# Attention stage of a decoder trunk: block splits on VectorE, state-space parameters on GpSimd, q and k norms folded into later scales, head products by weight block

## The chip, the core and the metric

The kernel runs on one core of a Trainium2 chip. A core has five engines with an instruction queue each: TensorE (PE; its weight loads are listed apart as PEld), VectorE (DVE), ScalarE (ACT), GpSimd (POOL) and SyncE (SP), which here issues most of the loads. The engines run side by side and meet only at semaphores; on one engine the instructions run in the order in which the program has them. The metric is device time in microseconds (us), the median of several runs; lower is better.

## The reference

Two layers of a decoder trunk on 256 tokens of width 1024, in float32. The first layer is RMSNorm, one input projection, two groups of eight attention heads, an output projection and a residual, then a dense SwiGLU (width 3584). The second is a state-space layer (complex diagonal, 32 groups of 64 states), then a top-2-of-8 expert SwiGLU. The change touches the first layer's attention and the small tables of the state-space layer. The attention, cut down:

```python
h = _rms_norm(x, norm_g) @ w_in                    # columns: q, k, v of the stick-breaking heads | c_q 256 | c_kv 128 | k_rope 32
o_sb = stick_breaking(q, k, v)                     # 8 heads of 64, causal, scale 1/8
c_q, c_kv = _rms_norm(..., q_lat_g), _rms_norm(..., kv_lat_g)
q = (c_q @ w_q_up)                                 # 8 heads of 64 + 32 (rotary)
kv = (c_kv @ w_kv_up)                              # 8 heads of 64 (k) + 64 (v)
k = concat([kv[..., :64], k_rope shared by all heads])
q, k = _rms_norm(q, q_g), _rms_norm(k, k_g)        # over 96, per head, each with a gain of 96
q, k = _rope_tail(q, cos, sin), _rope_tail(k, cos, sin)   # last 32 of 96
o_mla = softmax(q k^T * 96 ** -0.5, causal) @ v
x + concat(o_sb, o_mla) @ w_out
```

The state-space layer needs, of 2048 pairs of numbers a, dt, the values exp(a dt) with cosine and sine and a quotient; they depend on weights alone.

## The kernel before

**Products by three.** A float32 operand is held as a high and a low part. `mm3` (L247 to L249) forms a product from three: high by high, high by low, low by high. A weight block (1 MB, 128 x 2048) is loaded into one of five raw buffers; `split` (L226 on) makes its two parts in two halves of 1024 columns: ScalarE casts the high part `wh` (L218), and the engine given as `sub` subtracts for the low part `wl` (L219, `wl = raw - wh`). The pairs stand in a ring of six, so a half's buffers are reused three blocks later, when TensorE has read them; a raw buffer is free, and the next load in SyncE's order may start, once both halves are split.

**The stage in order.** (1) x is transposed and split into `xh`, `xl`; the latent columns (c_q, c_kv, k_rope) are computed from four narrow blocks `wc` of 416 columns, into PSUM tiles `pav`. (2) `r0` is the reciprocal root of each token's mean square; `dg` (L380, GpSimd) is a diagonal of it, which a product with ones (L416) turns into the row `rb`. `setup_late` loads the tables `cat` (masks, cosines, sines, gains) and `spar` (parameters of the state-space layer). (3) The latents `csb` are normed (L386 to L397). `s5_first` computes the first tables of the state-space layer in a scratch tile `kp`; it contains two exponentials by polynomial (`exp_exact`, L899). (4) `heads_T` (L408) forms the stick-breaking q, transposed, in PSUM, four products of 128 rows in two calls; L418 scales it into `qT`. Between the calls the latents are transposed into `cT`. (5) For each half b of the tokens, L468 and L472 form q, k and v of the latent heads, ScalarE copies them into `qk` and `vkv`, squares are summed (L479, L480), `norm(b)` computes the reciprocal root (L256 to L273) and multiplies `qk` by it (L448) and by the gains (L450), and `rope(b)` rotates the last 32 columns (L459 to L462). (6) `heads_T` forms k into `kT`, around `norm(1)`; `qk_T(b)` (L490) transposes `qk` into `qkT`. (7) The values of the stick-breaking heads (L627) are formed in two halves of the weights, with the scores of the first two heads (L518, L519, L512) between.

(8) The loop of L635 runs the sixteen heads as a pipeline written by hand: in each turn it issues steps of several heads, with the lags of the table `LAG`. A latent head: scores and mask (L545, L546, L512), maximum (L549, L550) and its negative scaled (L551), exponential with row sums (L554, L555), division (L560 to L562), transposition (L567, L571) and product with v (L580). A stick-breaking head: L523 to L526, a sum (L530), products with a triangle (L534, L535), exponential (L539), L580. Pairs are merged into `mh`, `ml` (L586, L587). (9) `out(n, half)` multiplies by the output weights; then follow the residual and the dense layer.

**What sets the order.** There is no planner: each engine runs its instructions in the order of the code, and the scheduling is by hand. The PSUM tiles named `pw` share four buffers, `ptr` and `pav` two each; a product into a fifth `pw` waits until the first has been read. SyncE issues the weight loads in a fixed order, each when its buffer is free.

**Who splits.** Of the four `wc` blocks VectorE splits one and GpSimd three. Of the eight wide blocks up to the second output block VectorE splits the first two (q) and GpSimd the other six (two k, two v, two output): `split(g)` at L398, L432, L496, L499, L502 and L630. VectorE splits all later ones. `s5_first` runs on VectorE, `s5_second` on GpSimd behind the loop of step (8).

Of the kernel before, what the change touches and what calls it, by code (L numbers as in the profile page):

```python
# [8 lines left out]
F32 = mybir.dt.float32  # L9
# [40 lines left out]
C_W = C_QG + 192  # L50
# [44 lines left out]
def lay_out(i):  # L95
# [17 lines left out]
    par[:, C_QG:] = np.concatenate([i["att_q_norm"][0], i["att_k_norm"][0]])  # L113
# [24 lines left out]
class Net:  # L138
# [211 lines left out]
    def attention(self, kp):  # L350
# [4 lines left out]
        with ExitStack() as st:  # L355
# [26 lines left out]
            self.split(v)  # L382
# [15 lines left out]
            self.split(g)  # L398
# [3 lines left out]
            self.s5_first(kp)  # L402
# [4 lines left out]

            def heads_T(W, dst, sc, m2):  # L408
                pq = bank([P, 2, SEQ])
                for mi in range(2):  # L410
                    for k in range(KD):
                        wh, wl = W[k]
                        s = slice((2 * m2 + mi) * P, (2 * m2 + mi + 1) * P)
                        self.mm3(pq[:, mi], wh[:, s], wl[:, s], xh[:, k], xl[:, k], k == 0, k == KD - 1)
                if dst is qT and m2 == 0:
                    mm(pr, self.ones, dg, start=True, stop=True)  # L416
                    act.copy(rb, pr)
                v.scalar_tensor_tensor(out=dst[:, 2 * m2:2 * m2 + 2], in0=pq, scalar=sc,  # L418
                                       in1=rb.unsqueeze(1).to_broadcast([P, 2, SEQ]), op0=ALU.mult, op1=ALU.mult)
# [11 lines left out]
            heads_T(W, qT, 0.125, 1)  # L431
            self.split(g)  # L432
# [6 lines left out]
            qg = self.cat[:, C_QG - C_A:C_QG - C_A + 192].rearrange("p (a c) -> p a c", a=2)  # L439
# [4 lines left out]

            def norm(b):
                qk = qks[b]
                r = self.rsqrt(ssq[b], 16, 1.0 / 96, sm=a2)
                v.tensor_tensor(out=qk, in0=qk, in1=r.unsqueeze(2).to_broadcast([P, 16, 96]), op=ALU.mult)  # L448
                for n in range(2):
# [1328 lines left out]
```

## Time and profile before

| | us |
|---|---|
| median of 3 runs | 1320.66 (1320.35 to 1320.78) |
| profiled execution, its own time | 1320.32 |
| span in the trace | 1318.2 |
| PE / PEld busy | 1269.5 / 920.8 |
| DVE / ACT / POOL busy | 842.5 / 632.9 / 219.4 |

The rest of an execution, 2.1 us, lies around the span. In a row of the timeline stand the start, the time in us, the engine, the line and operation, out<-in with the partitions and elements, the count of merged instructions, and in brackets the idle time of the engine before it with what ended it. Consecutive PE rows overlap, since products are pipelined: the distance from start to start is the rate. A row of the windows has the stretch, its length with PE busy, then PEld, DVE, ACT and POOL busy with their counts, the granted clock of TensorE as a share of full speed, the share of DMA and GB/s. A row of the waits has who waited for whom, the total, the times and the longest.

### The profile page before, as it was taken

The numbers are of one execution on the slowest core, as the hardware profiler recorded it, in microseconds if no ns is written. First come the engines' busy times: TensorE is split into PE (matmuls) and PEld (weight loads), VectorE is DVE, ScalarE is ACT, GpSimd is POOL, SyncE is SP. The second block draws the span as 40 slices with busy tenths as digits, with TensorE's granted clock in tenths as the row PEclk, the third lists the DMA queues.
The fourth block names the chain that finished last, engine by engine and source line by source line (L and its number), as shares of the span: only waits on it lengthen the run. The fifth ranks groups of instructions, "written<-read, shape, count | busy, mean of one in ns | idle before, by whom it ended". The sixth has DMA issues, their size and how long they took to land.

```text
span 1318.2 us, 18472 instructions
## 1 busy us (share of the span) xinstructions
PE 1269.5 (96%) x6862; PEld 920.8 (70%) x6862; DVE 842.5 (64%) x1108; ACT 632.9 (48%) x825; POOL 219.4 (17%) x257
## 2 busy tenths in 40 slices
PE   7789999999998889999999999999999999999997
PEld 7566999999987778884357885346887436788433
DVE  6876886856788589981158984128987106898211
ACT  6345544444452457771047773026876105777100
POOL 4454598001724600000000000000000000000000
PEclk9889999999999989999999999999999999999999
DMA  8330654545553759999999999999999999999996
GB/s 303 133 123 17 227 220 161 189 168 187 192 191 134 268 195 372 375 343 384 416 418 418 417 419 416 417 418 418 418 417 419 418 418 417 418 418 418 416 419 246
DMA packets 66369, 421.22 MB, mean 320 GB/s; under 512 B 7504, under 2 KB 8784, under 8 KB 21472
## 3 DMA queue, kind: packets, MB, share of 16 engines
q1 hardware_dynamic: 65088, 418.15, 79.9%
q10 hardware_dynamic: 1008, 1.27, 0.3%
q8 instruction: 56, 0.92, 0.3%
q0 software_dynamic: 176, 0.56, 0.1%
q14 instruction: 41, 0.34, 0.1%
HBM read 418.89 MB, written 1.05 MB: 319 GB/s over the span
## 4 chain that ended last, share of the span: by engine, by line


## 5 line engine op out<-in xcount | busy, mean ns | idle before, releaser
L219 DVE TENSOR_TENSOR wl<-raw,wh 128x1024 fp32r<-128x1024 f32 (+1 forms) x427 | 516.2, 1245 | 100.2 <-ACT wh L218 85.8
L218 ACT CAST wh<-raw 128x1024 fp32r<-128x1024 f32 (+1 forms) x456 | 467.2, 1046 | 180.9 <-PE dn L249 63.0
L693 PE MATMUL pgu<-raw,we 128*64 128x512 f32 x896 | 203.6, 596 | 0.0
L247 PE MATMUL pgu<-wh,wy 128*128 128x512 f32 x448 | 178.2, 398 | 0.0
L248 PE MATMUL pgu<-wl,wy 128*128 128x512 f32 x448 | 174.6, 390 | 1.0 <-DVE wl L219 1.0
L249 PE MATMUL pgu<-wh,wy 128*128 128x512 f32 x448 | 174.8, 390 | 0.0
L693 PEld LDWEIGHTS pgu<-raw,we 128*64 128x64 f32 x896 | 61.0, 137 | 115.5 <-issue 113.8
L247 PE MATMUL pgu<-dxh,wh 128*128 128x256 f32 x448 | 127.2, 284 | 0.0
L249 PE MATMUL pgu<-dxh,wl 128*128 128x256 f32 x448 | 126.8, 283 | 0.0
L248 PE MATMUL pgu<-dxl,wh 128*128 128x256 f32 x448 | 126.7, 283 | 0.0
L247 PE MATMUL dn<-wh,gh 128*128 128x512 f32 x280 | 109.8, 392 | 0.0
L249 PE MATMUL dn<-wh,gl 128*128 128x512 f32 x280 | 109.1, 390 | 0.0
L248 PE MATMUL dn<-wl,gh 128*128 128x512 f32 x280 | 109.0, 389 | 0.0
L727 PE MATMUL dn<-raw,gh 128*64 128x512 f32 x448 | 101.9, 593 | 0.5 <-ACT gh L713 0.5
L247 PEld LDWEIGHTS pgu<-wh,wy 128*128 128x128 f32 x448 | 84.1, 188 | 23.8 <-issue 4.7
L249 PEld LDWEIGHTS pgu<-wh,wy 128*128 128x128 f32 x448 | 84.1, 188 | 18.1
L248 PEld LDWEIGHTS pgu<-wl,wy 128*128 128x128 f32 x448 | 84.2, 188 | 17.9 <-DVE wl L219 1.4
L704 DVE TENSOR_TENSOR sg<-pgu,sg 64x512 f32<-64x512 f32 x28 | 19.4, 693 | 110.9 <-ACT sg L703 110.9
L713 ACT COPY gh<-pgt 128x256 f32<-128x256 f32 x28 | 10.4, 372 | 163.4 <-PE pgt L711 163.4
L247 PEld LDWEIGHTS pgu<-dxh,wh 128*128 128x128 f32 x448 | 85.9, 192 | 0.5 <-issue 0.2
L248 PEld LDWEIGHTS pgu<-dxl,wh 128*128 128x128 f32 x448 | 86.0, 192 | 0.3
L249 PEld LDWEIGHTS pgu<-dxh,wl 128*128 128x128 f32 x448 | 85.9, 192 | 0.0
(414 smaller groups left out, 1666.0 us busy)
## 6 DMA issues: line engine op xcount, KB each, us to landing
raw<-in_wm_dram SPq DMA_DIRECT2D x292, 1024.0 KB, 15.0
raw<-in_wm_dram SPq DMA_DIRECT2D x88, 512.0 KB, 15.0
raw<-in_wd_dram SPq DMA_DIRECT2D x42, 1024.0 KB, 4.9
raw<-in_wqkv_dram SPq DMA_DIRECT2D x6, 1024.0 KB, 5.9
raw<-in_wo_dram SPq DMA_DIRECT2D x4, 1024.0 KB, 4.9
raw<-in_wglu_dram SPq DMA_DIRECT2D x4, 1024.0 KB, 4.9
raw<-in_ws_dram SPq DMA_DIRECT2D x2, 1024.0 KB, 4.6
raw<-in_wc_dram SPq DMA_DIRECT2D x4, 416.0 KB, 6.7
```

The source lines that it names most:

```text
L218: self.nc.scalar.copy(wh, w)
L219: (sub or self.sub).tensor_tensor(out=wl, in0=w, in1=wh.bitcast(F32), op=ALU.subtract)
L247: mm(out, sh, mh, start=start, stop=False)
L248: mm(out, sh, ml, start=False, stop=False)
L249: mm(out, sl, mh, start=False, stop=stop)
L693: nc.tensor.matmul(pg[64 * j:64 * j + 64], x(k), W[j][0][k % 4], start=(k == 0), stop=(k == KD - 1))
L704: v.tensor_tensor(out=sg[:64], in0=pg[64:], in1=sg[:64], op=ALU.mult)
L713: nc.scalar.copy(g, pt)
L727: nc.tensor.matmul(job["acc"][64 * n:64 * n + 64], gts[0][:, k], W[n][0][k], start=(f == 0 and k == 0), stop=(f == NF - 1 and k == 3))
```

## The change

1. Every split of the stage is VectorE's. The split of the second q block stands ahead of `r0`'s chain instead of behind it, that of the first value block ahead of `rope(0)`, and that of the second output block moves from between the value halves to turn 16 of the loop.
2. `s5_first` runs on GpSimd, without its reciprocal. Operations that multiply and add two tiles in one instruction are written as two there. `s5_second` is called after `norm(1)` instead of behind the loop; the reciprocal is its first step, on VectorE.
3. `heads_T` goes through the weights once: each of its eight row blocks serves all four head products in turn, in two PSUM tiles open together. The latents' transposes come after row blocks 7 and 8 of q, the product for `rb` after the fifth.
4. `norm(b)` multiplies only the k half by its reciprocal root. The q half's goes, with 96 ** -0.5, into the scale of the exponential (L554, L555) and into the maximum (two instructions for L551's one). The gains of the first 64 columns become the scale of ScalarE's copy in `qk_T`; those of the last 32 are multiplied into the cosine and sine tables once, by six small products on GpSimd in `setup_late`. `rope(b)` takes q and k apart: seven instructions for four.

The order of instructions in three places. First VectorE, from the polynomial to the first sums of squares; before (`kp` is the scratch tile of the state-space tables, `pw` the q heads' PSUM tile):

```order
L911 TENSOR_SCALAR kp<-kp 128x16
L913 SCALAR_TENSOR_TENSOR kp<-kp 128x16 x6
L914 TENSOR_SCALAR kp<-kp 128x16
L915 TENSOR_SCALAR kp<-kp 128x16
L916 TENSOR_TENSOR kp<-kp 128x16
L418 SCALAR_TENSOR_TENSOR qT<-pw,rb 128x512 x2
L475 COPY qk<-csb 128x8x32
```

and with the change, from the latents' scales on:

```order
L408 TENSOR_SCALAR csb<-csb,rr 128x128
L222 TENSOR_TENSOR wl<-raw,wh 128x1024 x2
L432 SCALAR_TENSOR_TENSOR qT<-pw,rb 128x512 x2
L222 TENSOR_TENSOR wl<-raw,wh 128x1024 x2
L499 COPY qk<-csb 128x8x32
```

The tables have gone from ahead of the q evacuation, and a k block's split stands on either side of it.

Second GpSimd, after the masks' casts; before, twelve halves of weight blocks and then `s5_second`:

```order
L310 CAST mib<-cat 128x128
L219 TENSOR_TENSOR wl<-raw,wh 128x1024 x12
L962 TENSOR_SCALAR kp<-kp 128x16
L963 TENSOR_SCALAR kp<-kp 128x16
L966 COPY kp<-kp 128x16
```

and with the change:

```order
L313 CAST mib<-cat 128x128
L320 TENSOR_TENSOR gc<-cat 128x64
L320 TENSOR_TENSOR gs<-cat 128x2x16 x2
L320 TENSOR_TENSOR gc<-cat 128x64
L320 TENSOR_TENSOR gs<-cat 128x2x16 x2
L929 TENSOR_SCALAR kp<-kp 128x16
L930 TENSOR_SCALAR kp<-kp 128x16
```

The splits have left this queue; the tables with gains and `s5_first` (L929 on, 50 instructions) stand in their place, with `s5_second` directly behind.

Third VectorE at the end of the loop; before:

```order
L560 RECIPROCAL rs<-rs 128x2
L561 TENSOR_SCALAR p<-p,rs 128x128
L562 TENSOR_SCALAR p<-p,rs 128x256
L571 COPY pT<-ptr 128x384
L587 TENSOR_TENSOR ml<-pav,mh 128x256
```

and with the change:

```order
L584 RECIPROCAL rs<-rs 128x2
L585 TENSOR_SCALAR p<-p,rs 128x128
L586 TENSOR_SCALAR p<-p,rs 128x256
L222 TENSOR_TENSOR wl<-raw,wh 128x1024 x2
L595 COPY pT<-ptr 128x384
L611 TENSOR_TENSOR ml<-pav,mh 128x256
```

The second output block's split has come between the last division and the last copies.

The diff, without context lines (the host part, which appends two columns of gains to the table `par`, left out):

```diff
--- before
+++ after
...
@@ -311,0 +315,8 @@
+        self.gc, self.gs = (pool.tile([P, 2, 2, 32], F32, name=nm) for nm in ("gc", "gs"))
+        qg = self.cat[:, C_QG - C_A:C_QG - C_A + 192].rearrange("p (a c) -> p a c", a=2)
+        for b in range(2):
+            for o, c, d, w, s_ in ((self.gc, C_COS, 0, 32, 64), (self.gs, C_SIN, 0, 16, 80), (self.gs, C_SIN, 16, 16, 64)):
+                c += 32 * b + d - C_A
+                nc.gpsimd.tensor_tensor(out=o[:, b, :, d:d + w], in0=self.cat[:, c:c + w].unsqueeze(1).to_broadcast([P, 2, w]),
+                                        in1=qg[:, :, s_:s_ + w], op=ALU.mult)
@@ -369 +380 @@
-                self.split(v if i == 0 else g)
+                self.split(v)
@@ -374,0 +386 @@
+            self.split(v)
@@ -383 +394,0 @@
-            self.split(v)
@@ -398 +409,2 @@
-            self.split(g)
+            self.s5_first(kp)
+            self.split(v)
@@ -402 +413,0 @@
-            self.s5_first(kp)
@@ -408,12 +419,15 @@
-            def heads_T(W, dst, sc, m2):
-                pq = bank([P, 2, SEQ])
-                for mi in range(2):
-                    for k in range(KD):
-                        wh, wl = W[k]
-                        s = slice((2 * m2 + mi) * P, (2 * m2 + mi + 1) * P)
-                        self.mm3(pq[:, mi], wh[:, s], wl[:, s], xh[:, k], xl[:, k], k == 0, k == KD - 1)
-                if dst is qT and m2 == 0:
-                    mm(pr, self.ones, dg, start=True, stop=True)
-                    act.copy(rb, pr)
-                v.scalar_tensor_tensor(out=dst[:, 2 * m2:2 * m2 + 2], in0=pq, scalar=sc,
-                                       in1=rb.unsqueeze(1).to_broadcast([P, 2, SEQ]), op0=ALU.mult, op1=ALU.mult)
+            def heads_T(dst, sc, between=None):
+                pq = [bank([P, 2, SEQ]) for _ in range(2)]
+                for k in range(KD):
+                    if k % 4 == 0:
+                        W = self.takek(4, 0)
+                    wh, wl = W[k % 4]
+                    for m in range(4):
+                        s = slice(m * P, (m + 1) * P)
+                        self.mm3(pq[m // 2][:, m % 2], wh[:, s], wl[:, s], xh[:, k], xl[:, k], k == 0 and m % 2 == 0, k == KD - 1 and m % 2 == 1)
+                    if between:
+                        between(k)
+                for m2 in range(2):
+                    v.scalar_tensor_tensor(out=dst[:, 2 * m2:2 * m2 + 2], in0=pq[m2], scalar=sc,
+                                           in1=rb.unsqueeze(1).to_broadcast([P, 2, SEQ]), op0=ALU.mult, op1=ALU.mult)
@@ -421,2 +434,0 @@
-            W = self.takek(4, 0) + self.takek(4, 0)
-            heads_T(W, qT, 0.125, 0)
@@ -424 +436,8 @@
-            for b in range(2):
+            def latents_T(k):
+                if k == 4:
+                    mm(pr, self.ones, dg, start=True, stop=True)
+                    act.copy(rb, pr)
+                if k < 6:
+                    return
+                b = k - 6
@@ -431,2 +450,3 @@
-            heads_T(W, qT, 0.125, 1)
-            self.split(g)
+            heads_T(qT, 0.125, latents_T)
+            self.split(v)
@@ -439 +458,0 @@
-            qg = self.cat[:, C_QG - C_A:C_QG - C_A + 192].rearrange("p (a c) -> p a c", a=2)
@@ -444,0 +464,3 @@
+            rq = [ap.tile([P, 16], F32, name=f"rq{b}") for b in range(2)]
+            SC = 96 ** -0.5
@@ -446,6 +468,6 @@
-                qk = qks[b]
-                r = self.rsqrt(ssq[b], 16, 1.0 / 96, sm=a2)
-                v.tensor_tensor(out=qk, in0=qk, in1=r.unsqueeze(2).to_broadcast([P, 16, 96]), op=ALU.mult)
-                for n in range(2):
-                    v.tensor_tensor(out=qk[:, 8 * n:8 * n + 8], in0=qk[:, 8 * n:8 * n + 8],
-                                    in1=qg[:, n].unsqueeze(1).to_broadcast([P, 8, 96]), op=ALU.mult)
+                self.rsqrt(ssq[b], 16, 1.0 / 96, rq[b], sm=a2)
+                k = qks[b][:, 8:]
+                v.tensor_tensor(out=k, in0=k, in1=rq[b][:, 8:].unsqueeze(2).to_broadcast([P, 8, 96]), op=ALU.mult)
+                v.tensor_scalar(out=rq[b][:, :8], in0=rq[b][:, :8], scalar1=SC, scalar2=None, op0=ALU.mult)
@@ -453,0 +476,9 @@
+                qk = qks[b].rearrange("p (n h) c -> p n h c", n=2)
+                rt = ap.tile([P, 2, 8, 32], F32, tag="rt", name="rt")
+                bc = lambda t, c, w: t[:, b, :, c:c + w].unsqueeze(2).to_broadcast([P, 2, 8, w])
+                for n in range(2):
+                    for d, s_ in ((0, 80), (16, 64)):
+                        v.tensor_tensor(out=rt[:, n, :, d:d + 16], in0=qk[:, n, :, s_:s_ + 16],
+                                        in1=self.gs[:, b, n, d:d + 16].unsqueeze(1).to_broadcast([P, 8, 16]), op=ALU.mult)
+                    v.tensor_tensor(out=qk[:, n, :, 64:96], in0=qk[:, n, :, 64:96],
+                                    in1=self.gc[:, b, n].unsqueeze(1).to_broadcast([P, 8, 32]), op=ALU.mult)
@@ -455,8 +486 @@
-                rt = ap.tile([P, 16, 32], F32, tag="rt", name="rt")
-                cc = self.cat[:, C_COS - C_A + 32 * b:C_COS - C_A + 32 * b + 32]
-                ss = self.cat[:, C_SIN - C_A + 32 * b:C_SIN - C_A + 32 * b + 32]
-                for d, s_ in ((0, 80), (16, 64)):
-                    v.tensor_tensor(out=rt[:, :, d:d + 16], in0=qk[:, :, s_:s_ + 16],
-                                    in1=ss[:, d:d + 16].unsqueeze(1).to_broadcast([P, 16, 16]), op=ALU.mult)
-                v.tensor_tensor(out=qk[:, :, 64:96], in0=qk[:, :, 64:96], in1=cc.unsqueeze(1).to_broadcast([P, 16, 32]), op=ALU.mult)
-                v.tensor_tensor(out=qk[:, :, 64:96], in0=qk[:, :, 64:96], in1=rt, op=ALU.add)
+                v.tensor_tensor(out=qk[:, :, 64:96], in0=qk[:, :, 64:96], in1=rt.rearrange("p n h c -> p (n h) c"), op=ALU.add)
@@ -482,0 +507 @@
+            self.split(v)
@@ -491 +516,2 @@
-                    act.copy(qkT[:, 4 * q:4 * q + 4, blk[b]], pt[:96])
+                    n = C_QC - C_A + q // 2
+                    act.activation(qkT[:, 4 * q:4 * q + 4, blk[b]], pt[:96], AF.Copy, scale=self.cat[:96, n:n + 1])
@@ -493 +518,0 @@
-            W = self.takek(4, 0) + self.takek(4, 0)
@@ -495,2 +519,0 @@
-            heads_T(W, kT, 1.0, 0)
-            self.split(g)
@@ -498,2 +521,3 @@
-            heads_T(W, kT, 1.0, 1)
-            self.split(g)
+            self.s5_second(kp)
+            heads_T(kT, 1.0)
+            self.split(v)
@@ -502 +526 @@
-            self.split(g)
+            self.split(v)
@@ -507 +530,0 @@
-            SC = 96 ** -0.5
@@ -551 +574,2 @@
-                v.tensor_scalar(out=m, in0=m, scalar1=-SC, scalar2=None, op0=ALU.mult)
+                for b in range(2):
+                    v.tensor_scalar(out=m[:, b:b + 1], in0=m[:, b:b + 1], scalar1=rq[b][:, h:h + 1], scalar2=-1.0, op0=ALU.mult, op1=ALU.mult)
@@ -554,2 +578,2 @@
-                act.activation(p[:, 0:128], s[:, 0:128], AF.Exp, scale=SC, bias=m[:, 0:1], accum_out=rs[:, 0:1])
-                act.activation(p[:, 128:384], s[:, 128:384], AF.Exp, scale=SC, bias=m[:, 1:2], accum_out=rs[:, 1:2])
+                act.activation(p[:, 0:128], s[:, 0:128], AF.Exp, scale=rq[0][:, h:h + 1], bias=m[:, 0:1], accum_out=rs[:, 0:1])
+                act.activation(p[:, 128:384], s[:, 128:384], AF.Exp, scale=rq[1][:, h:h + 1], bias=m[:, 1:2], accum_out=rs[:, 1:2])
@@ -630 +653,0 @@
-                    self.split(g)
@@ -643,0 +667,2 @@
+                if i == n:
+                    self.split(v)
@@ -649 +673,0 @@
-            self.s5_second(kp)
@@ -903,2 +927,2 @@
-        xc, k, f, p, ki = mk("x"), mk("k"), mk("f"), mk("p"), mk("i", I32)
-        v = nc.vector
+        xc, k, f, p, t, ki = mk("x"), mk("k"), mk("f"), mk("p"), mk("t"), mk("i", I32)
+        v = nc.gpsimd
@@ -908,7 +932,8 @@
-        v.scalar_tensor_tensor(out=f, in0=k, scalar=-0.693359375, in1=xc, op0=ALU.mult, op1=ALU.add)
-        v.scalar_tensor_tensor(out=f, in0=k, scalar=2.12194440e-4, in1=f, op0=ALU.mult, op1=ALU.add)
-        co = [1.0 / 5040, 1.0 / 720, 1.0 / 120, 1.0 / 24, 1.0 / 6, 0.5, 1.0]
-        v.tensor_scalar(out=p, in0=f, scalar1=co[0], scalar2=None, op0=ALU.mult)
-        for c in co[1:]:
-            v.scalar_tensor_tensor(out=p, in0=p, scalar=c, in1=f, op0=ALU.add, op1=ALU.mult)
-        v.tensor_scalar(out=p, in0=p, scalar1=1.0, scalar2=None, op0=ALU.add)
+        for o, c, a in ((f, -0.693359375, xc), (f, 2.12194440e-4, f)):
+            v.tensor_scalar(out=t, in0=k, scalar1=c, scalar2=None, op0=ALU.mult)
+            v.tensor_tensor(out=o, in0=t, in1=a, op=ALU.add)
+        co = [1.0 / 5040, 1.0 / 720, 1.0 / 120, 1.0 / 24, 1.0 / 6, 0.5, 1.0, 1.0]
+        v.tensor_scalar(out=p, in0=f, scalar1=co[0], scalar2=co[1], op0=ALU.mult, op1=ALU.add)
+        for c in co[2:]:
+            v.tensor_tensor(out=p, in0=p, in1=f, op=ALU.mult)
+            v.tensor_scalar(out=p, in0=p, scalar1=c, scalar2=None, op0=ALU.add)
@@ -931 +956 @@
-        v = nc.vector
+        v = nc.gpsimd
@@ -943 +967,0 @@
-        v.reciprocal(self.den, self.den)
@@ -951,0 +976 @@
+        nc.vector.reciprocal(self.den, self.den)
```

More of the change, by code (lines that the diff above doesn't have):

```diff
@@ L49 @@
 C_QG = C_SIN + 64
-C_W = C_QG + 192
+C_QC = C_QG + 192
+C_W = C_QC + 2
 def host_consts():
@@ L112, in lay_out @@
     par[:, C_GN:C_L] = np.concatenate([col(nm) for nm, _ in GAINS], axis=1)
-    par[:, C_QG:] = np.concatenate([i["att_q_norm"][0], i["att_k_norm"][0]])
+    par[:, C_QG:C_QC] = np.concatenate([i["att_q_norm"][0], i["att_k_norm"][0]])
+    par[:, C_QC:] = 1.0
+    par[:64, C_QC:] = np.stack([i["att_q_norm"][0][:64], i["att_k_norm"][0][:64]], axis=1)
     o["par"] = par
@@ L416, in heads_T @@
+            cT = ap.tile([P, 3, SEQ], F32, name="cT")
+            def latents_T(k):
+                if k == 4:
                     mm(pr, self.ones, dg, start=True, stop=True)
                     act.copy(rb, pr)
-                v.scalar_tensor_tensor(out=dst[:, 2 * m2:2 * m2 + 2], in0=pq, scalar=sc,
-                                       in1=rb.unsqueeze(1).to_broadcast([P, 2, SEQ]), op0=ALU.mult, op1=ALU.mult)
-            W = self.takek(4, 0) + self.takek(4, 0)
-            heads_T(W, qT, 0.125, 0)
@@ L423, in attention @@
-            cT = ap.tile([P, 3, SEQ], F32, name="cT")
-            for b in range(2):
+                if k < 6:
+                    return
+                b = k - 6
                 pt = bank([P, 3, P], "tr", 2)
@@ L453, in rope @@
-            def rope(b):
-                qk = qks[b]
-                rt = ap.tile([P, 16, 32], F32, tag="rt", name="rt")
-                cc = self.cat[:, C_COS - C_A + 32 * b:C_COS - C_A + 32 * b + 32]
-                ss = self.cat[:, C_SIN - C_A + 32 * b:C_SIN - C_A + 32 * b + 32]
-                for d, s_ in ((0, 80), (16, 64)):
-                    v.tensor_tensor(out=rt[:, :, d:d + 16], in0=qk[:, :, s_:s_ + 16],
-                                    in1=ss[:, d:d + 16].unsqueeze(1).to_broadcast([P, 16, 16]), op=ALU.mult)
-                v.tensor_tensor(out=qk[:, :, 64:96], in0=qk[:, :, 64:96], in1=cc.unsqueeze(1).to_broadcast([P, 16, 32]), op=ALU.mult)
-                v.tensor_tensor(out=qk[:, :, 64:96], in0=qk[:, :, 64:96], in1=rt, op=ALU.add)
+                self.rsqrt(ssq[b], 16, 1.0 / 96, rq[b], sm=a2)
@@ new lines, in norm, with rope @@
+                k = qks[b][:, 8:]
+                v.tensor_tensor(out=k, in0=k, in1=rq[b][:, 8:].unsqueeze(2).to_broadcast([P, 8, 96]), op=ALU.mult)
+                v.tensor_scalar(out=rq[b][:, :8], in0=rq[b][:, :8], scalar1=SC, scalar2=None, op0=ALU.mult)
+            def rope(b):
+                qk = qks[b].rearrange("p (n h) c -> p n h c", n=2)
[7 more added lines that the diff above has]
+                                    in1=self.gc[:, b, n].unsqueeze(1).to_broadcast([P, 8, 32]), op=ALU.mult)
+                qk = qks[b]
+                v.tensor_tensor(out=qk[:, :, 64:96], in0=qk[:, :, 64:96], in1=rt.rearrange("p n h c -> p (n h) c"), op=ALU.add)
```

## The prediction

> **What bounds the kernel now.** I read the page's slices first, to see which stage has what limit.
>
> ```profile
> DMA  8330654545553759999999999999999999999996
> ```
>
> A slice is 33 us. From the 16th on the DMA engines are full: the expert stage streams weights. Before that TensorE is the engine to follow, and the diff touches only the attention, roughly the first four slices. So the question is when TensorE leaves that stage, and whether what follows keeps the gain. The timeline of TensorE there shows three long holes:
>
> ```profile
> 19.62 0.28 PE L247 MATMUL pw<-xh,wh 128*128 128x256 f32 x1
> ...
> 34.74 2.74 PE L468 MATMUL pw<-raw,cT 128*128 128x384 f32 x8
> 43.70 3.75 PE L472 MATMUL pw<-raw,cT 128*128 128x512 f32 x4 [6.22 <-issue]
> 47.24 3.31 PE L468 MATMUL pw<-raw,cT 128*128 128x384 f32 x8
> 50.39 1.88 PE L472 MATMUL pw<-raw,cT 128*128 128x512 f32 x4
> 51.71 0.68 PE L247 MATMUL pw<-xh,wh 128*128 128x256 f32 x1
> ...
> 63.49 0.28 PE L249 MATMUL pw<-xh,wl 128*128 128x256 f32 x1
> 67.29 0.64 PE L490 MATMUL ptr<-cst,qk 128*96 128x128 f32 x4 [3.52 <-DVE qk L462]
> ...
> 69.00 0.48 PE L247 MATMUL pw<-wh,xh 128*128 128x512 f32 x1
> ...
> 74.64 0.70 PE L518 MATMUL pw<-qT,kT 64*128 64x256 f32 x2
> ...
> 80.10 1.22 PE L518 MATMUL pw<-qT,kT 64*128 64x256 f32 x2 [4.32 <-DVE kT L418]
> ...
> 81.72 0.78 PE L247 MATMUL pw<-wh,xh 128*128 128x512 f32 x1
> ...
> 85.71 0.50 PE L247 MATMUL pw<-wh,xh 128*128 128x512 f32 x1
> ...
> 90.99 0.39 PE L545 MATMUL pw<-qkT 96*128 96x128 f32 x2
> ```
>
> The reader is to see that each hole ends on VectorE, though the first is marked "issue": L472 needs a PSUM buffer (four of that tag) whose last holder, the q-head product, is read by VectorE's L418. The next fence has why VectorE is late.
>
> ```profile
> 28.34 0.17 DVE L908 SCALAR_TENSOR_TENSOR kp<-kp 128x16 f32<-128x16 f32 x1
> 32.22 2.33 DVE L908 SCALAR_TENSOR_TENSOR kp<-kp 128x16 f32<-128x16 f32 x1
> 32.11 9.31 POOL L219 TENSOR_TENSOR wl<-raw,wh 128x1024 fp32r<-128x1024 f32 x4
> 42.92 1.28 DVE L418 SCALAR_TENSOR_TENSOR qT<-pw,rb 128x512 f32<-128x512 f32 x2
> ...
> 58.83 10.62 POOL L219 TENSOR_TENSOR wl<-raw,wh 128x1024 fp32r<-128x1024 f32 x4 [17.40 <-ACT wh L218]
> 61.71 2.77 DVE L461 TENSOR_TENSOR qk<-qk,cat 128x512 f32<-128x512 f32 x1
> 80.74 0.69 DVE L461 TENSOR_TENSOR qk<-qk,cat 128x512 f32<-128x512 f32 x1
> ```
>
> The same 16-column instruction takes 0.17 us alone and 2.33 us beside GpSimd's subtraction, which is also about 2.33 us long (9.31 / 4): VectorE sits out whole GpSimd instructions. It holds for L461 too (0.69 against 2.77). So the cost of GpSimd's splits is not their own length but what they do to VectorE, and L418, the rotation and the k evacuation stand behind it in VectorE's order. The windows show a second price:
>
> ```profile
> 40.00:50.00 10.00, 6.30 (x11) 3.13 (x12) 5.25 (x14) 3.13 (x7) 1.43 (x1) 0.66 0.40 144
> 80.00:90.00 10.00, 9.90 (x41) 8.14 (x42) 4.69 (x10) 6.45 (x11) 4.66 (x2) 0.70 0.01 2
> 90.00:100.00 10.00, 10.00 (x58) 7.20 (x57) 6.98 (x23) 5.37 (x15) 7.46 (x32) 1.00 0.31 105
> ```
>
> In the windows of the 6.22 and the 4.32 us hole the granted clock is 0.66 and 0.70 instead of 1.00, so the work behind a hole runs slow as well.
>
> **Term 1: the holes and the slow work behind them.** First: 6.2 us idle; then 3.54 us (43.70 to 47.24) for four products whose second turn takes 1.32 (50.39 to 51.71), 2.2 lost; then 3.15 for what took 2.74 before the hole, 0.4 lost: 8.8. Second: 3.5. Third: 4.3 idle; then nine products take 3.99 (81.72 to 85.71) where 24 take 5.64 (69.00 to 74.64), 2.1 for nine, 1.9 lost: 6.2. Four small waits on the first head weights:
>
> ```profile
> PE pw L249 <- DVE wl L219: 1.5, 4, 0.9
> ```
>
> Together 8.8 + 3.5 + 6.2 + 1.5 = 20.0 us, if nothing new appears.
>
> The Trainium skill bears on the slow work: its page "TensorE: Matmul & The Clock Gate" (Part 1) says the array falls back to half rate after some microseconds idle and needs about 3.4 us of work to recover. The 3.52 us hole, with a rate of 0.23 us per product right behind it, did not show this, the other two did. Were the slow work not given back, the gain would be 2.2 + 0.4 + 1.9 = 4.5 us smaller.
>
> **Do new waits replace them?** All block splits of the stage are VectorE's now; I laid its new order out from rows (line numbers are those before).
>
> ```profile
> 19.66 4.72 DVE L219 TENSOR_TENSOR wl<-raw,wh 128x1024 fp32r<-128x1024 f32 x4
> 50.76 0.17 DVE L256 TENSOR_SCALAR rx<-ssq 128x16 f32<-128x16 f32 x1
> 53.05 1.76 DVE L448 TENSOR_TENSOR qk<-qk,rr 128x1536 f32<-128x1536 f32 x1
> 54.84 1.83 DVE L450 TENSOR_TENSOR qk<-qk,cat 128x768 f32<-128x768 f32 x2
> 19.72 5.05 POOL L380 TENSOR_SCALAR dg<-cst,r 128x128 f32<-128x128 f32 x2 [1.76 <-DVE r L273]
> ```
>
> A block costs 2.35 us (two halves of 1.18). A norm falls from 2.3 (reciprocal root, 50.76 to 53.05) + 1.76 + 1.83 to 2.3 + 0.9 (half of 1.76) + 0.2, by 2.5. A rotation's five pieces come to about 2.4 with nothing beside it (one piece of 512 columns is 0.69). s5_first leaves. VectorE then has hardly a gap from 17 to 61 us: first q block and r0 to 22.4, second q block and latent scales to 28, first k block to 30.4, q evacuation 31.8 to 33.0, second k block to 35.7, norm(0) 37 to 42, sums of squares to 44.4 (paced by ScalarE), first value block to 46.7, rope(0) to 49.1, norm(1) and the reciprocal to 52.7, k evacuation to 54.0, second value block to 56.3, rope(1) to 58.7, first output block to 61.1.
>
> TensorE without holes, by the quoted rates (96 head products in 11.8 us, 51.71 to 63.49) from a head start at 19.1: q heads with the latent turns to 32.1, L468 and L472 to 40.2 (twice 2.74 + 1.32), k heads to 52.0, qk_T(0) to 53.7 (67.29 to 69.00 is 1.7), values to 59.4, two scores to 61.2 (under 1 each), values to 64.0, qk_T(1) to 65.7, values to 68.5. What VectorE owes is there each time: the q evacuation, which frees L472's buffer, 1.8 us ahead, rope(0) 2.9, k evacuation 5.4, second value block 4.9, rope(1) 5.3. So L545 moves from 90.99 to 68.5, a gain of 22.5; the holes alone gave 20.0. I take **21.3** between them.
>
> What is doubtful: dg on GpSimd. Its two instructions took 5.05 us beside VectorE's splits; they begin at 22.4, TensorE wants them at 26.2. Cost 0 (only one block stands beside them now) to 1.3; with the short margins of 1.8 and 2.9 I take **1.0**, bounds 0 to 3.
>
> Weight loads need no term: the value blocks are wanted at 43 and 46 and their buffers come free at 25 and 30.4. In SyncE's order the tables (cat, spar) stand one load later, behind the first q block's split at 19.1; GpSimd, their first reader, is by then not past dg.
>
> **Term 2: parameters on GpSimd.** s5_first becomes 50 small instructions there, six table products stand ahead, s5_second follows. The 90 to 100 window gives 7.46 us for 32, 0.23 busy and about 0.31 from one to the next: 15 us, from about 36 to 51. VectorE's reciprocal (L943 before) now needs the 28th, at about 45, and is reached at 52.4: cost 0, covered by 7 us. Without that cover the k evacuation, the second value block and rope(1) queue behind it.
>
> By the Trainium skill's page "SBUF — State Buffer" (Who interferes with whom), a VectorE instruction with two SBUF inputs and a GpSimd instruction that reads SBUF exclude one another for the whole of an instruction. The rows at 32 us agree. This speaks against the change in one respect: GpSimd's small steps now meet VectorE's 1.18 us subtractions. By it the 28 steps would lose about 1 us at each of two splits, 47 instead of 45.
>
> **Term 3: the last block.** The second output block's split leaves GpSimd for VectorE, ahead of the last copies of the softmax phase.
>
> ```profile
> 121.61 0.35 DVE L562 TENSOR_SCALAR p<-p,rs 128x256 f32<-128x256 f32 x1
> 123.46 0.41 DVE L587 TENSOR_TENSOR ml<-pav,mh 128x256 fp32r<-128x256 f32 x1
> 122.71 0.48 PE L247 MATMUL pw<-wh,mh 128*128 128x512 f32 x1
> ```
>
> The split stands between these two VectorE rows, on today's clock: the last ml, ready at 123.87, moves by 2.35 to 126.2. The output products start at 122.71 and reach it at their twelfth (0.23 each), 125.3: 0.9 lost, more if ScalarE's two casts, also new there, come late. I take **1.5**, bounds 0 to 2.5. The two pT copies are wanted only behind all 24 products, at 128.3: covered.
>
> **Term 4: two scale steps per head instead of one.**
>
> ```profile
> 99.92 0.17 DVE L551 TENSOR_SCALAR mx<-mx 128x2 f32<-128x2 f32 x1
> 99.99 0.56 DVE L530 TENSOR_TENSOR sp<-sp,sa 128x384 f32<-128x384 f32 x1
> 109.43 0.91 PE L534 MATMUL pw<-sp,cat 128*128 128x384 f32 x2 [0.60 <-DVE sp L530]
> ```
>
> One step is 0.07 to 0.2 us, eight heads 0.6 to 1.6; it stands ahead of L530, for which TensorE waited at 109.43. I take **0.5**, bounds 0 to 1.6.
>
> **Sum.** 21.3 − 1.0 − 1.5 − 0.5 = 18.3. The profiled execution took 1320.32 us around a span of 1318.2, so it becomes 1302.0; the median stands 0.34 above it: 1320.66 − 18.3 = **1302.4**.
>
> **Rivals.** (a) *VectorE becomes the bound.* For: no gap from 17 to 61 us. Against: its reserve is some 5 us late in the stage. If short GpSimd steps cost some 40 VectorE instructions 0.3 us each, it is 12 late, TensorE 7: about 1309.5. The 90 to 100 window, with GpSimd busy and L530 at its usual 0.56, speaks against that.
>
> (b) *The weight stream keeps the gain:* 1320.
>
> ```profile
> 480.00:500.00 20.00, 19.04 (x86) 15.38 (x86) 19.41 (x30) 16.49 (x18) 0.00 (x0) 1.00 0.69 256
> SPq L184 <- DVE wl L219: 435.8, 123, 42.7
> ```
>
> For: DMA is full for the last 60%. Against: it is at 0.69 just before that, and the load queue's greatest wait is for a split to free a buffer. The stream starts when the stage before lets it, so it moves along.
>
> (c) *Slower:* the reciprocal is reached before GpSimd has its input. VectorE stands there until step 28; TensorE loses all beyond 5 us of that. It decides once a step takes more than (52.4 + 5 + 18.3 − 36) / 28 = 1.42 us. For it:
>
> ```profile
> 201.28 1.20 POOL L926 TENSOR_TENSOR rot<-rot,we 128x16 f32<-128x16 f32 x1
> ```
>
> a 16-column step of 1.20 beside VectorE's splits; but its neighbours are 0.22 to 0.25. At 1.6 us each the time is 1320.66 + 28 × (1.6 − 1.42) = 1325.7.
>
> **Chances.** The forecast 0.70, (a) 0.18, (b) 0.06, (c) 0.06. The forecast alone spans 1298.2 (gain 22.5, no losses) to 1307.8 (20.0 and every loss at its upper end, 7.1); the range reaches into (a): 1297.5 to 1310.5. A difference under 0.2% (2.6 us) cannot be told from none here. Faster 0.88, same 0.06, slower 0.06.
>
> **What would show it.** Right: L472 without the 6 us hole, qk_T(0) and the first scores without waits on VectorE, the first latent scores (L545) at 68 to 72 us, clock 1.00 from 20 us on, the q normaliser gone from VectorE, and the later stages the same length, moved. Term 3 right: a TensorE wait of 1 to 2 us on ml in the first output products. Wrong: VectorE instructions still two or more times their lone length between 20 and 60 us, the reciprocal with a wait, or an expert stage longer than before.

## The result and the profile after

The changed kernel takes 1300.04 us (1297.54 to 1300.62) against 1320.51 us (1318.16 to 1320.78) of the kernel before, run beside it: a ratio of 0.9848 (95% interval 0.9834 to 0.9862). The profiled execution took 1299.78 us with a span of 1297.7, so 20.5 us less than before in the same terms. Forecast were 1302.4 us, 18.3 less.

The timeline of TensorE, changed kernel. The lines have moved: L247, L249, L468, L472, L490, L518 and L545 before are now L250, L252, L492, L496, L515, L541 and L568.

```profile
26.09 0.60 PE L439 MATMUL pw<-dg,ones 128*128 128x256 f32 x2
...
31.48 2.75 PE L492 MATMUL pw<-raw,cT 128*128 128x384 f32 x8
34.07 1.88 PE L496 MATMUL pw<-raw,cT 128*128 128x512 f32 x4
35.78 2.74 PE L492 MATMUL pw<-raw,cT 128*128 128x384 f32 x8
38.36 1.88 PE L496 MATMUL pw<-raw,cT 128*128 128x512 f32 x4
...
51.59 0.60 PE L515 MATMUL ptr<-cst,qk 128*96 128x128 f32 x4
...
58.88 0.70 PE L541 MATMUL pw<-qT,kT 64*128 64x256 f32 x2
...
68.16 0.39 PE L568 MATMUL pw<-qkT 96*128 96x128 f32 x2
...
100.20 0.48 PE L250 MATMUL pw<-wh,mh 128*128 128x512 f32 x1
...
104.02 0.50 PE L252 MATMUL pw<-wh,ml 128*128 128x512 f32 x1 [1.02 <-DVE ml L611]
```

None of the three holes is left, and the first latent scores stand at 68.16 instead of 90.99 us. From 20 to 130 us TensorE waits for another engine only this often (who waited for whom, total, times, longest):

```profile
PE pw L557 <- DVE sp L553: 1.2, 2, 0.6
PE pw L252 <- DVE ml L611: 1.0, 1, 1.0
PE ptr L591 <- DVE p L585: 0.6, 1, 0.6
PE pgu L250 <- DVE h L679: 0.5, 1, 0.5
```

The first and the third were there before with 1.2 and 0.5; those for ml and h are new. Where the gain arose, from start to start on TensorE:

| stretch | before | after | gained |
|---|---|---|---|
| until the q heads start | 19.62 | 18.90 | 0.7 |
| q heads | 15.12 | 12.58 | 2.5 |
| latent products, until the k heads | 16.97 | 8.20 | 8.8 |
| k heads, until the transposes of qk | 15.58 | 11.91 | 3.7 |
| until the first scores | 7.35 | 7.29 | 0.1 |
| scores and values, until the latent scores | 16.35 | 9.28 | 7.1 |
| softmax loop, until the output products | 31.72 | 32.04 | −0.3 |
| first output products, until the last product with v | 5.77 | 7.05 | −1.3 |
| until the dense layer's product for its norm | 33.8 | 34.6 | −0.7 |

The 20.5 us come out at the end whole. The windows of the changed kernel, first a piece of the attention, then the attention and the expert stage:

```profile
30.00:40.00 10.00, 10.00 (x40) 6.05 (x38) 6.92 (x13) 8.43 (x20) 7.37 (x23) 1.00 0.59 211
...
0.00:130.00 130.00, 121.05 (x702) 98.99 (x703) 98.70 (x247) 78.35 (x171) 53.73 (x162) 1.00 0.48 178
...
580.00:1280.00 700.00, 697.19 (x3291) 426.22 (x3292) 379.38 (x397) 321.56 (x368) 0.00 (x0) 1.00 1.01 416
```

and of the kernel before, the attention, which takes some 20 us more, and the expert stage, 20 us later:

```profile
0.00:150.00 150.00, 126.75 (x698) 101.31 (x699) 110.74 (x251) 76.56 (x170) 67.46 (x123) 0.95 0.42 151
...
600.00:1300.00 700.00, 697.19 (x3292) 426.63 (x3292) 379.78 (x397) 320.95 (x367) 0.00 (x0) 1.00 1.01 416
```

In windows 20 us apart the expert stage shows the same count of products (3292 and 3291 records), the same busy time and the same 416 GB/s: it is as long as before and begins earlier. The granted clock of the attention is 1.00 instead of 0.95.

VectorE and GpSimd of the changed kernel, in the stretch that was laid out in the prediction:

```profile
21.87 3.28 POOL L392 TENSOR_SCALAR dg<-cst,r 128x128 f32<-128x128 f32 x2 [20.92 <-DVE r L276]
30.70 1.34 DVE L432 SCALAR_TENSOR_TENSOR qT<-pw,rb 128x512 f32<-128x512 f32 x2 [0.29 <-PE pw L252]
33.53 2.47 DVE L222 TENSOR_TENSOR wl<-raw,wh 128x1024 fp32r<-128x1024 f32 x2 [1.48 <-ACT wh L221]
35.01 1.24 POOL L929 TENSOR_SCALAR kp<-kp 128x16 f32<-128x16 f32 x1
44.86 1.29 POOL L967 TENSOR_TENSOR kp<-kp 128x16 f32<-128x16 f32 x1
49.00 0.69 DVE L486 TENSOR_TENSOR qk<-qk,rt 128x512 f32<-128x512 f32 x1
52.92 0.24 DVE L976 RECIPROCAL kp<-kp 128x16 f32<-128x16 f32 x1
58.99 2.35 DVE L222 TENSOR_TENSOR wl<-raw,wh 128x1024 fp32r<-128x1024 f32 x2
```

VectorE runs at its lone lengths (the rotation's sum 0.69, as at 80.74 before), and it is the short GpSimd steps that are held for a VectorE subtraction now (1.24 and 1.29 instead of some 0.25). The first output block's split ends at 61.3; the layout had 61.1.

### The profile page after: what moved, and what is told of

It reads as the page before. It is cut to its first block, busy times and chain, and to the rows that moved or that the text cites. A ratio compares the mean times of both kernels' runs of the same rounds, so it can differ in the third digit from the quotient of the medians.

```text
span 1297.7 us, 18489 instructions
## 1 busy us (share of the span) xinstructions
PE 1263.9 (97%) x6862; PEld 918.6 (71%) x6862; DVE 829.0 (64%) x1102; ACT 634.9 (49%) x825; POOL 205.2 (16%) x295
## 3 DMA queue, kind: packets, MB, share of 16 engines
q10 hardware_dynamic: 1008, 1.27, 0.3%
## 4 chain that ended last, share of the span: by engine, by line
## 5 line engine op out<-in xcount | busy, mean ns | idle before, releaser
L222 DVE TENSOR_TENSOR wl<-raw,wh 128x1024 fp32r<-128x1024 f32 (+1 forms) x445 | 533.5, 1235 | 103.1 <-ACT wh L221 90.3
L250 PE MATMUL pgu<-wh,wy 128*128 128x512 f32 x448 | 178.2, 398 | 0.0
L252 PE MATMUL pgu<-wh,wy 128*128 128x512 f32 x448 | 174.8, 390 | 0.0
L250 PE MATMUL pgu<-dxh,wh 128*128 128x256 f32 x448 | 127.3, 284 | 0.5 <-DVE h L679 0.5
L252 PE MATMUL pgu<-dxh,wl 128*128 128x256 f32 x448 | 126.8, 283 | 0.0
L250 PE MATMUL dn<-wh,gh 128*128 128x512 f32 x280 | 109.8, 392 | 0.0
L252 PE MATMUL dn<-wh,gl 128*128 128x512 f32 x280 | 109.1, 390 | 0.0
L250 PEld LDWEIGHTS pgu<-wh,wy 128*128 128x128 f32 x448 | 84.2, 188 | 23.8 <-issue 4.7
L252 PEld LDWEIGHTS pgu<-wh,wy 128*128 128x128 f32 x448 | 84.1, 188 | 18.2
L250 PEld LDWEIGHTS pgu<-dxh,wh 128*128 128x128 f32 x448 | 85.9, 192 | 1.1 <-DVE h L679 0.7
L252 PEld LDWEIGHTS pgu<-dxh,wl 128*128 128x128 f32 x448 | 85.9, 192 | 0.0
```

The lines of the kernel that those rows point to most:

```text
L222: (sub or self.sub).tensor_tensor(out=wl, in0=w, in1=wh.bitcast(F32), op=ALU.subtract)
L250: mm(out, sh, mh, start=start, stop=False)
L252: mm(out, sl, mh, start=False, stop=stop)
```

## Experiments

Two theories. **A**: VectorE was late since each GpSimd subtraction of a split kept it standing, so the gain comes with the splits' departure from GpSimd. **B**: VectorE was late by the sum of its own work, so the gain comes with what leaves it, the state-space tables and half of the norms. Ratios below are to the kernel before, run beside each; 0.001 is 1.3 us.

**e1: the kernel before, all splits on VectorE, at their old places.**

```diff
-                self.split(v if i == 0 else g)
+                self.split(v)
...
-            self.split(g)
+            self.split(v)
```

The second pair stands for all six places.

> The kernel before with one part of the change alone: all nine block splits that GpSimd had are VectorE's, at their old places; the state-space tables, norms and head products are as before. Theory A (VectorE is held up by whole GpSimd subtractions): VectorE gets 14 us of work more and yet the stage ends earlier; the first hole shrinks to some 2 us, the third one goes; 1304 to 1309 us. Theory B (VectorE is relieved by what leaves it, the tables and half of the norms): with more work and no relief no gain, 1318 to 1328 us.

Measured: 1310.79 us, 0.9939 (0.9920 to 0.9958), 1.8 us above the range of A. VectorE got 17 us more work there (six wide blocks of 2.35 and three narrow ones of 1.1) and the kernel became 8 us faster, which B excludes. The three holes are gone but for 0.3 us of the first (k heads at 43.2, transposes at 55.2). But one wait is new:

```profile
PE pw L545 <- ACT vsb L633: 7.6, 1, 7.6
```

So without GpSimd's subtractions the holes go, but that gives less than half of the gain: something else is late at the end of the values.

**e2: e1, and GpSimd subtracts for nobody.** Where each wide block's split stood on GpSimd, it now does four subtractions of 128 x 512 into a tile that nobody reads, 24 in all.

```diff
+            idle = ap.tile([P, 512], F32, name="idle")
+            def also():
+                for x in (0, 512, 0, 512):
+                    g.tensor_tensor(out=idle, in0=self.h[:, 0, x:x + 512], in1=self.h[:, 1, x:x + 512], op=ALU.subtract)
...
-            self.split(g)
+            self.split(v)
+            also()
```

> As the run with VectorE's splits alone, and GpSimd subtracts for nothing: 24 instructions of 128x512 on the input, into a tile that nobody reads, behind its table casts, some 27 us from about 32 us on. Nobody waits for them. Theory A: VectorE's 16-column steps take about 1 us each beside them and the gain goes again: 12 to 25 us above the run without them. Theory B: within 1.5 us of it.

Measured: 1331.91 us, 1.0096 (1.0078 to 1.0115); the span is 21.1 us over e1's. No engine needs what GpSimd computes there. The timeline of GpSimd and VectorE, and TensorE's longest wait:

```profile
31.50 34.42 POOL L379 TENSOR_TENSOR idle<-h 128x512 f32<-128x512 f32 x24
41.24 1.12 DVE L919 TENSOR_SCALAR kp<-kp 128x16 f32<-128x16 f32 x1
42.39 0.17 DVE L920 SCALAR_TENSOR_TENSOR kp<-kp 128x16 f32<-128x16 f32 x1
42.60 1.12 DVE L921 SCALAR_TENSOR_TENSOR kp<-kp 128x16 f32<-128x16 f32 x1
43.76 0.17 DVE L923 TENSOR_SCALAR kp<-kp 128x16 f32<-128x16 f32 x1
43.97 4.06 DVE L925 SCALAR_TENSOR_TENSOR kp<-kp 128x16 f32<-128x16 f32 x6
...
50.45 1.28 DVE L425 SCALAR_TENSOR_TENSOR qT<-pw,rb 128x512 f32<-128x512 f32 x2
```

```profile
PE pw L480 <- issue: 14.0, 1, 14.0
```

Steps of 0.17 us take 1.12 in turn with 0.17, the six of the polynomial 4.06 instead of e1's 1.27, and the hole ahead of the second latent product is back with 14 us. This shows A's mechanism by itself. It does not show its size in the kernel before, whose subtractions came in shorter rows (9.3 us from 32.11, 10.6 from 58.83, the rest later) and not in one of 34.

**e4: the kernel before, the state-space tables alone on GpSimd.**

```diff
-        v = nc.vector
+        v = nc.gpsimd
```

in `exp_exact` and `s5_first`, with the steps written in two as in the change, and the reciprocal on VectorE behind.

> The kernel before with s5_first on GpSimd alone, splits on GpSimd as before. VectorE is relieved of some 20 us (the time that s5_first took there, most of it waiting). Theory A: the first hole goes, but s5_first stands ahead of the second k block's split on GpSimd, TensorE waits for that in the k heads: 1317 to 1326 us. Theory B: relief of VectorE is the gain, 1308 to 1313 us.

Measured: 1322.94 us, 1.0023 (1.0013 to 1.0033): nothing won, 3 us lost. The first hole is gone here as well (k heads at 42.9, before at 51.7). But the tables stand between two splits in GpSimd's queue, and the wait has gone over to the second of these:

```profile
PE pw L249 <- POOL wl L219: 14.5, 2, 13.9
```

The time is in A's range and B's is missed, but by this new wait. So the run does not separate the theories: the first hole goes when either side of the meeting is taken away, GpSimd's subtractions (e1) or VectorE's small steps (e4). Against B as the whole cause stand e1 and e2.

**e3: e1 and the tables on GpSimd (e4's edit).**

> The kernel before with two parts: all splits on VectorE at their old places, and s5_first on GpSimd, called where it was; norms, head products and s5_second's place as before. Theory A: the first hole goes as well, 1301 to 1304 us, so that norms, weight order and moved splits together are worth 1 to 4 us. Theory B: the norms are a good part of the gain, so over 1306.

Measured: 1310.54 us, 0.9932 (0.9914 to 0.9949): not to be told from e1. It is above A's range; it is within B's "over 1306", but the norms, B's reason, are not what TensorE waits for here. The k heads start only 0.7 us earlier than in e1 (42.5), and the same wait stays, with 7.8 us. The timeline of VectorE and ScalarE ahead of it:

```profile
69.14 0.55 DVE L524 SCALAR_TENSOR_TENSOR sa<-sp,pw 128x384 f32<-128x384 f32 x1
71.78 2.41 DVE L219 TENSOR_TENSOR wl<-raw,wh 128x1024 fp32r<-128x1024 f32 x2 [2.08 <-ACT wh L218]
74.69 0.55 DVE L524 SCALAR_TENSOR_TENSOR sa<-sp,pw 128x384 f32<-128x384 f32 x1
75.28 0.52 ACT L525 ACTIVATE sa<-sa 128x384 f32<-128x384 f32 x1 [2.58 <-DVE sa L524]
78.16 1.28 ACT L633 ACTIVATE vsb<-pw,r 128x512 f32<-128x512 f32 x2
```

The second output block's split stands between the first steps of the two heads. It waits 2.08 us for ScalarE's cast, which itself stands behind the first head's L525 and L526; the second head's L524 comes behind the split, L525 behind that, and the copy of the values, for which TensorE waits, behind them all. So the last move in piece 1 of the change, that of this split into turn 16, was the suspect.

**e5: e3 with only that split moved.**

```diff
-                    self.split(v)
...
+                if i == n:
+                    self.split(v)
```

> The kernel before with all splits on VectorE and the state-space tables on GpSimd (as e3), and the second output block's split taken from between the value halves to turn 16 of the loop. If that split's old place made TensorE's wait of 7.8 us on the values' copy (ScalarE's vsb): the wait falls to under 3 us, the first latent scores come at 72 to 74 us instead of 78.9, and the time is 1304 to 1306 (4.5 to 6 us under e3). If VectorE is late there through the longer norms and the two calls per head product instead: the wait stays above 5 us and the time is 1309 to 1311.

Measured: 1305.55 us, 0.9887 (0.9873 to 0.9902), 6 us under e3 by the ratios.

```profile
PE pw L545 <- ACT vsb L632: 3.0, 1, 3.0
```

The wait fell from 7.8 to 3.0. The latent scores came at 75.0, 3.9 earlier, but a little later than the 72 to 74 expected: VectorE was still late. The rest of the 6 us lies behind the hole: in e3 the granted clock there is 0.50 (78 to 82 us), in e5 it stays at 1.00. The move of one split, which the prediction had down as a loss of 1.5, is worth 6 us once all splits are VectorE's.

**u1, u2, u3: the changed kernel with one part undone each**: the first tables back on VectorE; the norms as before; the head products in two calls. Their diffs are the change's own pieces 2, 4 and 3, reversed; u1 leaves `s5_second` and the reciprocal where the change put them.

> The changed kernel with s5_first back on VectorE, in its old instructions, at its new place ahead of the first k block's split. Its 34 steps take about 0.2 us each with no GpSimd subtraction beside them, 7 us, and the q evacuation behind them comes at 38 instead of 30.7 us; L496 waits for a PSUM buffer some 4 us, and VectorE's later reserve of 2 to 3 us takes up part of the rest. Theory A: 1304 to 1306.5 us. Theory B (what left VectorE is the gain): 1310 or more.

> The changed kernel with norm, rotation, exponential and transposed copies as before (q is multiplied by its reciprocal root and its gains again, one scale step per head). VectorE gets 2.5 us more per half of the tokens. Its reserve at rope(0) is 1.9 us, at rope(1) 4.6: TensorE waits 0.5 to 2 us, and gets 0.3 back in the loop. Theory A: 1300 to 1302 us. Theory B: 1305 or more.

> The changed kernel with the head products in two calls again, each through the whole weights. Then the second q block is wanted after 12 products instead of 48, at about 20.5 us, and is split at 23.0 and 24.2: TensorE waits 2.5 to 3.5 us in the q heads, and the latents' transposes may catch up some of it. 1302 to 1304 us. If the order of the weights mattered for the ring of buffers (the k and value blocks split late), 1306 or more.

| | time, us | ratio | first latent scores, us |
|---|---|---|---|
| changed kernel | 1300.04 | 0.9848 (0.9834 to 0.9862) | 68.2 |
| u1 tables on VectorE | 1302.40 | 0.9868 (0.9853 to 0.9883) | 71.4 |
| u2 norms as before | 1302.83 | 0.9876 (0.9861 to 0.9891) | 71.3 |
| u3 heads in two calls | 1302.51 | 0.9870 (0.9855 to 0.9885) | 72.5 |

By the trace each part undone costs 3 to 4 us up to the latent scores; the ratios, 2.6 to 3.7 us apart from the changed kernel's, say the same with intervals that overlap it. u3 is within the range expected; u1 came out lower than A's range, u2 0.8 us higher than it. None of the three stalls where before did. The waits name the new place, first u1, then u2, then u3:

```profile
PE pw L250 <- ACT qk L493: 1.4, 1, 1.4
```

```profile
PE pw L557 <- ACT vsb L644: 2.9, 1, 2.9
```

```profile
PE pw L252 <- DVE wl L222: 2.7, 2, 2.6
```

In u1 the q evacuation comes at 37.41 instead of 30.70, and TensorE waits for ScalarE's copies of the latent heads, 1.4 us and once more 0.7, where 4 us were expected. In u2 the longer norms make VectorE, and behind it ScalarE's copy of the values, late; in u3 TensorE reaches the second q block after 12 products instead of 48, and stands for its split. So the tables, the norms and the order of the head products are each needed for the layout to close without a wait.

**i1: the changed kernel, the second output block's split two turns later**, behind the last `ml`.

```diff
-                if i == n:
-                    self.split(v)
                 if i == n + 2:
+                    self.split(v)
                     out(0, 0)
```

> The changed kernel with the second output block's split two turns later, behind the loop's last ml that the first output products read. The wait of 1.02 us on ml goes; the split is done at about 104.5 us, wanted at 108: 1299.0 us, 0.08% below the changed kernel. If the split only moves the wait to the second half of the products, no gain or up to 1 us slower.

Measured: 1297.40 us, 0.9834 (0.9820 to 0.9847). Run again, beside the changed kernel on one chip:

> i1 once more, beside the changed kernel on the same chip. If the 1.2 us that its trace won is the split's place: 1 to 1.5 us under the changed kernel. If the difference of the first comparison was between chips: equal within 0.5.

> The changed kernel once more, as the base of i1 on the same chip: 0.985 of the kernel before; nothing is to be told apart by it alone.

Measured: i1 1298.23 us, 0.9830 (0.9817 to 0.9844), the changed kernel 1299.07 us, 0.9835 (0.9822 to 0.9849). The timeline of VectorE in this run of i1:

```profile
100.52 0.41 DVE L611 TENSOR_TENSOR ml<-pav,mh 128x256 fp32r<-128x256 f32 x1
100.93 2.36 DVE L222 TENSOR_TENSOR wl<-raw,wh 128x1024 fp32r<-128x1024 f32 x2
```

The last `ml` is ahead of the split, and the wait for it is gone from TensorE's list. From the start of the q heads to the dense layer's norm TensorE takes 121.7 us instead of 123.0: 1.3 us, in both pairs of runs. The whole times agree in sign (0.8 us here), but their intervals overlap; it is the fastest version found, with i2 its equal.

**i2: i1 with one scale step per latent head instead of two.**

```diff
-                for b in range(2):
-                    v.tensor_scalar(out=m[:, b:b + 1], in0=m[:, b:b + 1], scalar1=rq[b][:, h:h + 1], scalar2=-1.0, op0=ALU.mult, op1=ALU.mult)
+                v.tensor_tensor(out=m, in0=m, in1=nq[:, h], op=ALU.mult)
```

> i1 (second output block's split two turns later) with one scale step for the maximum of a latent head instead of two: the negated reciprocal roots of q are written once per half into a tile of head by half, and one product of two columns takes the two steps' place. If the two steps cost what the loop's length shows (32.0 us instead of 31.7): 0.3 us less than i1, which the times cannot tell apart; the loop is 31.7 long in the trace. If they cost the 0.5 us of the prediction or more: 31.5 or less. If nothing: 32.0.

Measured: 1297.96 us, 0.9827 (0.9814 to 0.9840). The loop is 32.03 us long against 32.10 of i1 beside it: the second step cost nothing that can be seen.

## Why the prediction was right, and where its sizes were off

The sign, the place and the mechanism held, and the time fell inside the range. Step by step, in us:

| step | predicted | measured |
|---|---|---|
| term 1, to the first latent scores | 21.3 (holes 20.0, layout 22.5) | 22.8 |
| dg | −1.0 | 0 |
| term 2, tables on GpSimd | 0, 28th step at 45 | 0, at 46.2 |
| term 3, the split in turn 16 | −1.5 | −1.3 |
| term 4, two scale steps | −0.5 | 0 (i2) |
| rest of the loop | 0 | −0.3 |
| behind the output products | 0 | −0.7 |
| sum | 18.3 | 20.5 |

**Term 1** was mis-sized by taking the middle. The layout was right to 0.3 us; the count of the holes was short by 2.8. Against its pieces the table of stretches has 8.8 (counted 8.8), 3.7 (3.5), 7.1 (6.2), 2.5 in the q heads (1.5), and 0.7 by which these start earlier. The last has 0.4 of a wait for a narrow block's split on GpSimd, which was not counted. In the q heads the four waits cost 2.5 from start to start (19.73 to 21.16 for two products instead of 0.24, and so on), where the idle times add up to 1.5: rows of products overlap, and the idle time begins only when the last row has ended. In the third stretch the scores right behind the hole were left out: 1.62 us (80.10 to 81.72) for what takes 0.88 in e1. Both ends stood in the prediction, and there was no reason for the mean: once VectorE's new order met every due time, the layout was the estimate and the holes only a floor.

**dg** cost nothing: its two instructions took 3.28 us, not 5.05, and were done at 25.15 for the product at 26.09. The margin of 0.9 us is thin, but it was there. The upper bound of 3 had no row behind it; the working beside it gives 1.3.

**Term 2** held. The 28th GpSimd step ended at 46.15 and the reciprocal ran at 52.92 without a wait. By the rule of the Trainium skill's page "SBUF — State Buffer" (Who interferes with whom) the prediction named 47 instead, with two steps blocked for a subtraction each; the trace shows two such among the 28, of 1.24 and 1.29 us, and a third of 0.87 beside the norm's product (L472, two SBUF inputs, 0.96), and agrees with the rule.

**Term 3** held in place and size for the changed kernel. What the term left out is the other side: by e3 and e5 the split's old place costs some 6 us once VectorE has it. In the prediction this gain sits unseen in the layout, which simply has no split there.

**Term 4** was charged by its instruction's length. The loop did grow by 0.3 us, but i2, which takes the second step out again, is no shorter. Where the 0.3 comes from stays open. One thing more is longer in the loop, which the prediction did not price: ScalarE's exponentials, whose scale is now a column of a tile, take 0.46 and 0.56 us instead of 0.37 and 0.47. No run tried them alone. Of the 0.7 us behind the output products 0.5 is the new wait for the residual `h`; why VectorE is late there was not tried.

That the sum comes so near is in part luck: three terms were too careful by 1.5, 1.0 and 0.5 us, and against that 1.0 us was lost where the prediction had no term.

**Rivals.** (a), VectorE as the bound, falls: VectorE's small steps kept their 0.17 to 0.22 us beside GpSimd's short ones, and its table of times was met within 0.3 us at the end. (b), the weight stream, falls: the expert stage moved whole. (c), a late reciprocal, falls: a step took (46.15 − 35.01) / 28 = 0.40 us, not 1.42. Of the signs of being wrong one shows, in a single small step: L261 at 24.97 took 0.36 us instead of 0.17, beside the end of dg; TensorE did not wait for it. All marks named as right appeared: the clock is 1.00, the scores come at 68.2 (68 to 72 forecast), and ml makes TensorE wait 1.02.

The prediction did not say how the gain divides, and here the experiments correct the picture that its profile lines suggest. Taking the subtractions off GpSimd is worth 8 us alone (e1), not the 20 of the holes; with the tables and the one moved split 15 (e5). The other 5 come from the rest of the change together: the norms and the order of the head products (u2, u3), and the new places of `s5_second` and of two more splits, which no run tried alone. So A names what made the holes of the kernel before (e1, e2), and B a smaller part, the last few us, where VectorE's own work sets the time (u1, u2). The parts do not add: the tables alone lose 3 us, are worth nothing behind e1, and some 3 us in the full change (u1).

## What to carry to other kernels

When an engine's small steps show two lengths, look at what the neighbour on the shared path does, and price a piece of work by whom it stops, not by its own time. Then write the engine's whole new order with due times: a change of several parts pays in full only when every due time is met, and single parts, tried alone, may show nothing or a loss. A bulky step without a due time of its own belongs behind the short steps that others wait for.

## What the runs showed of the hardware

**The blocking goes in turns, and by kind of instruction.** Beside a continuous row of GpSimd subtractions (e2) VectorE's dependent steps did not all wait: lengths mostly alternate, 1.12 and 0.17 us. So engines do not meet only at semaphores, as the opening has it: nothing that GpSimd did there was waited for by a semaphore. It caught instructions with a single tile input too: L919 above, 1.12 us for 16 columns, and a copy from SBUF:

```profile
55.05 1.36 DVE L483 COPY qk<-csb 128x256 f32<-128x256 f32 x1
56.44 1.90 DVE L488 TENSOR_REDUCE ssq<-sq 128x8 f32<-128x768 f32 x2
```

The same instructions in the timeline of e1, where GpSimd had no subtractions (L475 and L480 are L483 and L488 of e2):

```profile
35.08 1.27 DVE L913 SCALAR_TENSOR_TENSOR kp<-kp 128x16 f32<-128x16 f32 x6
36.77 1.28 DVE L418 SCALAR_TENSOR_TENSOR qT<-pw,rb 128x512 f32<-128x512 f32 x2
...
40.24 0.30 DVE L475 COPY qk<-csb 128x256 f32<-128x256 f32 x1
40.97 1.81 DVE L480 TENSOR_REDUCE ssq<-sq 128x8 f32<-128x768 f32 x2 [0.43 <-ACT sq L479]
```

The copy was held, the reductions were not, and neither was L425, which reads PSUM and one SBUF tile (1.28 in both). The Trainium skill's page "SBUF — State Buffer" (Who interferes with whom) says that copies and scalar steps can take both ports and then contend, while reductions on this chip never do; the traces agree with each.

**A shorter hole can cost the clock when a longer one doesn't.** In the kernel before, 3.52 us without work ahead of the transposes left the granted clock at 1.00. Its windows, the hole and what follows:

```profile
64.00:66.00 2.00, 0.00 (x0) 0.00 (x0) 1.97 (x2) 0.00 (x0) 2.00 (x1) 1.00 0.56 98
...
68.00:70.00 2.00, 2.00 (x16) 1.83 (x15) 1.93 (x5) 2.00 (x5) 1.45 (x1) 1.00 0.05 21
```

Nor did e5's hole of 3.04 us lower it. In u3 a hole of 2.58 us did, though not at once:

```profile
22.00:24.00 2.00, 0.98 (x6) 0.78 (x6) 1.99 (x2) 2.00 (x10) 2.00 (x1) 0.97 0.97 395
24.00:26.00 2.00, 1.95 (x9) 1.96 (x10) 1.57 (x9) 2.00 (x4) 1.83 (x4) 0.50 0.81 187
26.00:28.00 2.00, 2.00 (x14) 2.00 (x14) 1.83 (x10) 0.04 (x1) 0.00 (x0) 0.67 0.97 397
```

The work resumed at 22.91 and ran at full rate until about 24, then for some 3.3 us at a granted clock of 0.50, with 0.21 us from product to product instead of 0.12. Some 13 products at that rate cost 1.2 us; with the wait of 2.6 this is most of the 4.3 us at the latent scores (72.48 against 68.16). Length alone does not decide; what does was not tried.
